# Layer 1's FFN way out by seven block products for eight, in two passes over pairs of F-tiles

## The chip, the cores and the metric

The kernel runs on one core of a Trainium2 chip. The metric is the device time of one execution in microseconds, from the median of three runs. A difference between two kernels is read in per cent of that time.

A core has five engines that work side by side, each with its own queue of instructions, and wait for each other by semaphores: TensorE (PE in the profile, with its weight loads as PEld) multiplies matrices into PSUM, VectorE (DVE), ScalarE (ACT) and GpSimd (POOL) work element by element on SBUF and PSUM, and SyncE (SP) issues the DMA transfers between DRAM and SBUF. PSUM has eight banks of 128 x 512 float32.

## The reference

Two layers of a diffusion backbone over 512 latent tokens and 256 context tokens of width 1024: layer 0 has windowed and dense attention, layer 1 differential attention, and each layer ends with a SwiGLU FFN of hidden width 2816. Only the last step of layer 1 is concerned here, where the context tokens have dropped out:

```python
def _swiglu(h, w_in, w_out):
    gate, up = jnp.split(h @ w_in, 2, axis=-1)
    return (jax.nn.silu(gate) * up) @ w_out
...
        x = x + gx2 * _swiglu(_rms(x, norm_ffn_w[l]) * (1.0 + scx2) + shx2, ffn_w_in[l], ffn_w_out[l])
```

The way out is the product with `w_out`: 512 tokens x 2816 hidden columns by 2816 x 1024, in float32.

## The kernel before

Float32 products run as three products of the matrix engine's fp32r type. Every operand is cut into a high part, which ScalarE casts, and a low part, which VectorE (or GpSimd) makes by subtracting the high part from the operand; then high x high, high x low and low x high are added up in PSUM. `split_into` (L961) makes such a pair: a cast (L963) and a subtraction (L964). `unit` (L360) does the same for a weight that it loads (L364, L369, L370).

The hidden width is cut into NF = 22 F-tiles of 128. In layer 1, `gate_up_blocks` (L818) makes the hidden activations, transposed, F-tile by F-tile. It already multiplies blocks in the Winograd way: seven block products P1 to P7 of 256 tokens by half the model width for eight, whose operands are the blocks B11, B21, B12, B22 of the normed input (in the two `hT` tiles) and the combinations T1 to T4 (T1 in the pool `hop`, T2 and T3 in the former context room, T4 in the place of B12). In each F-tile the order on the matrix engine is P1, P5, P4 of the F-tile before, P6, P2, P7, P3; the last F-tile's P4 ends the stage. Weight tiles `wr`, and the combinations `ws` in PSUM, are cut into `wbh` and `wbl` (L866, L876), nine of each in a ring; of the subtractions, GpSimd makes G2's low part (L876) and S3 (L852), VectorE the rest. The product of gate and up (L929) is written into `hid`, a tile of four F-tiles by 512 tokens; all six such tiles stay in SBUF.

`way_out1` (L1014) then runs over the 22 F-tiles once. For each, `ready_hid` (L1022) loads 128 x 1024 of `ffn_w_out`, cuts it into `wdh` and `wdl` and cuts the hidden F-tile into `hdh` and `hdl`. The first two F-tiles are cut into the places of B11, B21 and T2, which come free while the last F-tile of the gate/up blocks still runs; the others have five buffers. `sums` (L1037) adds up the F-tile's part of all eight output tiles (four token tiles by two halves of the width), each in a PSUM bank of its own: 8 x 3 = 24 matmuls (L1041, L1042, L1043) of 128 x 128 by 512 columns. The last four F-tiles are held back and run bank by bank, so that `residual` (L469: times the gate, L472, plus x, L473) and the store (L1056) of one bank lie beside the products of the next.

The order on the matrix engine is written out by hand (`manual_schedule`); on all other engines a planner with a cost model of its own orders the instructions of the whole program ahead of time, by the order in which the code names them and by when it thinks them ready. `behind(...)` puts an instruction behind a named earlier one in that order. Pools are taken in stack order; a new pool's tiles wait, tile by tile, for those whose memory they take.

Of the kernel before, what the change touches and what calls it, by code (L numbers as in the profile page):

```python
# [18 lines left out]
P = 128  # L19
# [43 lines left out]
def backbone(es: ExitStack, tc: tile.TileContext, x, c, ctx, c_ctx, mod_w, mod_b, norm_mix_w, norm_ffn_w,  # L63
# [25 lines left out]
    def raw_tile(shape, name):  # L89
        return keep.tile(shape, F32, name=name, tag="raw", bufs=2)  # L90
# [24 lines left out]
    def f32(ap):  # L115
        return ap.bitcast(F32)
# [698 lines left out]

        return first_raw

    def gate_up_blocks(l, N, H, order, first_raw, next_raw, ring, ahead, early, tmp, deep, hid, singles, z, after, done=None):  # L818

        raw, sums, ops, psum, tmps = {}, {}, {}, {}, {}  # L820

# [58 lines left out]
        def bank(f, i):  # L880
            if (f, i) not in psum:
                b = i if isinstance(i, int) else i[0]
                psum[f, i] = z("pz") if b == 2 else singles.pool.tile([P, 512], F32, name=f"p{b}", tag=f"p{b}", bufs=2)
            return psum[f, i]

        def product(f, p):
# [21 lines left out]
            def gates():  # L908
                if (f, "cg") not in tmps:
                    tmps[f, "cg"] = tmp.tile([P, 2 * N], F32, name="cg", tag="cg", bufs=deep)  # L910
                return tmps[f, "cg"]

            if p == "P1":
                copied("s1")
            elif p == "P5":
                copied("s5")
            elif p == "P6":
                copied("s2")
            elif p in ("P2", "P3"):
                a, s = (0, "s1") if p == "P2" else (1, "s2")  # L920
                nc.vector.tensor_add(gates()[:, a * N:(a + 1) * N], ps, tmps[f, s])
# [39 lines left out]
    def split_into(to, src):  # L961
        hi, lo = to
        nc.scalar.copy(hi, src)  # L963
        nc.vector.tensor_sub(lo, src, f32(hi))  # L964
# [46 lines left out]
                residual(xs[t], banks[i], g[0 if t < NTX else 1], n)  # L1011
                done(t, n)

    def way_out1(xs, hidr, pool, places_w, places_h):  # L1014

        banks = [p_1.tile([P, 512], F32, name="dps", tag=tag) for tag in ("tr0", "tr1", "acc0", "acc1")]
        banks += [singles.pool.tile([P, 512], F32, name="dps", tag=tag, bufs=2) for tag in ("p0", "p0", "p1", "p1")]
        places = [(t, n) for t in range(NTX) for n in range(2)]
        held = 4
        ready = {}  # L1020

        def ready_hid(f):  # L1022
            def views(raw):
                yield raw, ffn_w_out[1, f * P:(f + 1) * P, :]
            if f < len(places_w):
                raw = raw_tile([P, D], "wdr")
                turn["load"] = nc.sync.dma_start(raw, ffn_w_out[1, f * P:(f + 1) * P, :])
                w, h = places_w[f], places_h[f]
                split_into(w, raw.rearrange("p (k c) -> p k c", k=4))
                split_into(h, hidr[f].rearrange("p (k c) -> p k c", k=2))  # L1030
            else:
                w = [z.rearrange("p (k c) -> p k c", k=4) for z in unit(pool, views, [P, D], 5, "wd")]
                h = [pool.tile([P, 2, SEQ // 2], F32R, name=name, tag=name, bufs=5) for name in ("hdh", "hdl")]
                split_into(h, hidr[f].rearrange("p (k c) -> p k c", k=2))
            ready[f] = h, w

        def sums(f, i):  # L1037
            (t, n), ps = places[i], banks[i]
            hh, hl = (z[:, t // 2, t % 2 * P:(t % 2 + 1) * P] for z in ready[f][0])
            a, b = (z[:, 2 * n:2 * n + 2, :] for z in ready[f][1])  # L1040
            nc.tensor.matmul(ps, hh, a, start=f == 0, stop=False)  # L1041
            nc.tensor.matmul(ps, hh, b, start=False, stop=False)  # L1042
            nc.tensor.matmul(ps, hl, a, start=False, stop=f == NF - 1)  # L1043

        g = gate_row(1, 5, 0, pool)
        for f in range(NF - held):
            ready_hid(f)
            for i in range(len(places)):
                sums(f, i)
        for f in range(NF - held, NF):  # L1050
            ready_hid(f)
        for i, (t, n) in enumerate(places):
            for f in range(NF - held, NF):
                sums(f, i)
            residual(xs[t], banks[i], g, n)
            nc.sync.dma_start(out[0, t * P:(t + 1) * P, n * 512:(n + 1) * 512], xs[t][:, n * 512:(n + 1) * 512])  # L1056

    class Pairs:

# [355 lines left out]
    with tc.manual_schedule(engines={mybir.EngineType.PE}):  # L1415
# [101 lines left out]
        states[0].close()  # L1517
        at.close()
        low = Pool("hid_low")
        hidr = {}  # L1520
# [33 lines left out]
    singles = Pool("singles1", space=PSUM)  # L1554
    high = Pool("hid_high")
    first.append(slot("first1", high, (P, 4, 4, P), F32R))
    ring = Pool("ring1")
    hop = Pool("hop1")
    tmp = Pool("tmp1")
    half = SEQ // 2  # L1560

    def hid_group(f):
        new = slot("hid", high if f in (0, 16, 20) else low)
        hidr.update({f + j: new[:, j] for j in range(4)})

    tc2 = ctx_room([P, KT, TOK - SEQ], F32R, "hTt")
    t1 = [hop.pool.tile([P, 4, half], F32R, name=f"t1{j}") for j in range(2)]
# [31 lines left out]

    with tc.manual_schedule(engines={mybir.EngineType.PE}):  # L1600
        gate_up_blocks(1, half, H, block_order(last_norm, differences, last_difference), first_raw, next_raw, ring.pool, 9, early,
                       tmp.pool, 2, hid_room, singles, acc_tile, "scaled2")
        tmp.close()
        hop.close()
        ring.close()
        g2 = Pool("g2")
        way_out1(xs, hidr, g2.pool, [H["B11"], H["B21"]],
                 [[z[:, 2 * j:2 * j + 2] for z in H["T2"]] for j in range(2)])
    g2.close()
    high.close()  # L1610
    low.close()
# [58 lines left out]
```

## Time and profile before

| | us |
|---|---|
| median of 3 runs | 1728.59 |
| runs | 1728.57 to 1735.44 |
| profiled execution | 1730.63 |
| its span, first to last instruction | 1728.5 |
| granted clock of the matrix engine, mean | 0.989 |
| way out of layer 1, first to last product | 1604.4 to 1724.1 |

In the rows of the profile an instruction stands with its line, its engine and `out<-in` by the names of tiles. Rows of a stretch (A:B, then the length) give the busy time and number of instructions of each engine, in the order of the header row: PE, PEld, DVE, ACT, POOL, then the granted clock of the matrix engine, the mean busy share of the DMA engines and GB/s. Rows of groups give shapes, a count, the busy time, the mean duration in ns, and the idle time before them with what ended it. Rows of a timeline give start and duration in us, and in brackets the idle time before. Rows of one line give count, and shortest, median and longest duration in ns.

### The profile page before, as it was taken

Reading aid. Unit: us, or ns where it says so; the run is one execution under the profiler, and the core shown is the slowest. Engines: PE = TensorE matmul, PEld = TensorE weight load, DVE = VectorE, ACT = ScalarE, POOL = GpSimd, SP = SyncE. Lnnn points to the kernel's source line nnn. Section 1 sums busy time; section 2 is a strip of 40 time slices with the busy share of each in tenths; the row PEclk is TensorE's granted clock in tenths of the full one; section 3 lists DMA queues with packets and bytes.
Section 4 is the critical chain, followed back from the end, with each engine's and each line's share of the span. In section 5 each row is a group of like instructions: output and inputs, shape, how many; then the busy total and the mean of one; then the engine's idle time right before and its main releaser. Section 6 shows DMA issues by size and latency. Waiting matters only on the chain. (4 is left out here: it accounts for less than half of the span.)

```text
span 1728.5 us, 28553 instructions
## 1 busy us (share of the span) xinstructions
PE 1661.1 (96%) x10378; PEld 1478.9 (86%) x10378; DVE 1134.9 (66%) x1993; ACT 936.2 (54%) x2010; POOL 720.8 (42%) x867
## 2 busy tenths in 40 slices
PE   6999999999999999999999899999997999999998
PEld 3887777677999999998777789999986799999887
DVE  3765655534899887757766656666675398887433
ACT  5555655734555665545564456666664465555321
POOL 1774554723345554303413466666653242222000
PEclk8999999999999999999999999999999999999999
DMA  9112322401355555449945212111113143332431
GB/s 319 53 42 62 96 88 82 147 28 51 116 172 174 167 158 158 130 123 345 299 153 172 99 44 75 41 45 46 34 37 98 32 143 102 106 107 57 137 96 67
DMA packets 217964, 194.64 MB, mean 113 GB/s; under 512 B 20000, under 2 KB 202592, under 8 KB 217824
## 3 DMA queue, kind: packets, MB, share of 16 engines
q1 hardware_dynamic: 217472, 192.62, 36.2%
q8 instruction: 81, 1.33, 0.3%
q14 instruction: 59, 0.48, 0.1%
q10 hardware_dynamic: 352, 0.21, 0.0%
HBM read 179.91 MB, written 12.87 MB: 112 GB/s over the span
## 5 line engine op out<-in xcount | busy, mean ns | idle before, releaser
L866 ACT CAST wbh<-wr 128x512 fp32r<-128x512 f32 x170 | 105.1, 621 | 132.9 <-PE p L898 72.1
L898 PE MATMUL p<-hT,wbh 128*128 128x256 f32 (+1 forms) x752 | 156.0, 301 | 0.0
L465 PE MATMUL inps<-wih,hT 128*128 128x384 f32 x384 | 136.1, 354 | 6.5 <-ACT qkv L667 6.0
L876 POOL TENSOR_TENSOR wbl<-wr,wbh 128x512 fp32r<-128x512 f32 x43 | 59.2, 1376 | 174.6 <-ACT wbh L866 170.7
L467 PE MATMUL inps<-wih,hT 128*128 128x384 f32 x384 | 131.3, 342 | 0.0
L466 PE MATMUL inps<-wil,hT 128*128 128x384 f32 x384 | 130.9, 341 | 0.0
L898 PEld LDWEIGHTS p<-hT,wbh 128*128 128x128 f32 x752 | 123.1, 192 | 0.2
L876 DVE TENSOR_TENSOR wbl<-wr,wbh 128x512 fp32r<-128x512 f32 x127 | 106.1, 844 | 20.0 <-ACT wbh L866 16.5
L898 PE MATMUL p<-hT,wbl 128*128 128x256 f32 (+1 forms) x376 | 112.9, 300 | 1.8 <-POOL wbl L876 1.8
L898 PE MATMUL p<-t,wbh 128*128 128x384 f32 (+1 forms) x480 | 111.0, 317 | 0.0
L370 POOL TENSOR_TENSOR wil<-wir,wih 128x768 fp32r<-128x768 f32 x44 | 82.4, 1873 | 51.7 <-ACT wih L369 51.0
L230 POOL TENSOR_TENSOR modp<-modp 128x512 f32<-128x512 f32 x40 | 55.9, 1398 | 115.1 <-ACT modp L229 115.1
L898 PE MATMUL p<-hTt,wbh 128*128 128x256 f32 (+1 forms) x480 | 101.3, 303 | 0.0
L852 POOL TENSOR_TENSOR wr<-wr 128x512 f32<-128x512 f32 x40 | 61.1, 1528 | 92.7 <-DVE ws L857 84.8
L898 PE MATMUL p<-b,wbh 128*128 128x384 f32 x368 | 94.7, 339 | 0.2 <-DVE c L926 0.2
L866 ACT CAST wbh<-ws 128x512 fp32r<-128x512 f32 x120 | 69.6, 581 | 43.2 <-PE p L898 29.2
L595 POOL TENSOR_SCALAR Pt<-Pt,rc 128x256 f32<-128x256 f32 (+3 forms) x96 | 69.3, 734 | 55.8 <-DVE rc L592 48.6
L223 DVE SCALAR_TENSOR_TENSOR ma<-modw,cols,ma 128x256 f32<-128x256 f32 x140 | 89.7, 641 | 2.3
L465 PEld LDWEIGHTS inps<-wih,hT 128*128 128x128 f32 x384 | 72.6, 189 | 12.7 <-ACT qkv L667 8.5
L585 ACT ACTIVATE Pt<-sc,nm 128x256 f32<-128x256 f32 (+3 forms) x96 | 67.8, 711 | 28.7 <-DVE nm L581 14.8
L898 PEld LDWEIGHTS p<-t,wbh 128*128 128x128 f32 x480 | 82.9, 189 | 0.0
L876 DVE TENSOR_TENSOR wbl<-ws,wbh 128x512 fp32r<-128x512 f32 x120 | 81.6, 680 | 1.7 <-ACT wbh L866 1.6
(332 smaller groups left out, 5277.2 us busy)
## 6 DMA issues: line engine op xcount, KB each, us to landing
modw<-in_mod_w_dram SPq DMA_DIRECT2D x96, 512.0 KB, 4.6
wr<-in_ffn_w_in_dram SPq DMA_DIRECT2D x176, 256.0 KB, 3.0
wdr<-in_ffn_w_out_dram SPq DMA_DIRECT2D x66, 512.0 KB, 4.1
wir<-in_od_w_in_dram SPq DMA_DIRECT2D x96, 128.0 KB, 2.3
hidm<-hid SPq DMA_DIRECT2D x44, 192.0 KB, 4.0
hr<-hidm SPq DMA_DIRECT2D x22, 192.0 KB, 4.0
x<-in_x_dram SPq DMA_DIRECT2D x8, 512.0 KB
wir<-in_ev_w_in_dram SPq DMA_DIRECT2D x16, 256.0 KB, 3.3
```

Of the source, the lines that this page charges most:

```text
L223: nc.vector.scalar_tensor_tensor(acc, w[:, k], scale[k], acc, ALU.mult, ALU.add)
L230: nc.gpsimd.tensor_add(pr[:, 0:2], pr[:, 0:2], pr[:, 2:4])
L370: (sub or nc.vector).tensor_sub(lo, raw, f32(hi))
L465: nc.tensor.matmul(ps, hs[0][:, k, :], a, start=k == 0, stop=False)
L466: nc.tensor.matmul(ps, hs[0][:, k, :], b, start=False, stop=False)
L467: nc.tensor.matmul(ps, hs[1][:, k, :], a, start=False, stop=k == KT - 1)
L585: turn["exp"] = nc.scalar.activation(p[:, :n], s, AF.Exp, bias=nm[:, c1], accum_out=sm[:, c1])
L595: nc.gpsimd.tensor_scalar(p[:, :n], p[:, :n], rc[:, hh:hh + 1], 1.0, ALU.mult, ALU.mult)
L852: nc.gpsimd.tensor_sub(w, raw[f, "G1"], w)
L866: nc.scalar.copy(hi, w)
L876: (nc.gpsimd if name == "G2" else nc.vector).tensor_sub(lo, raw[need[n]], f32(hi))
L898: nc.tensor.matmul(ps, w[:, k, :], H[b][h][:, k, :], start=first and k == 0 and q == 0, stop=final and k == 3 and q == 2, skip_group_check ...
```

## The change

`way_out1` is written anew. Each step takes a pair of F-tiles (f and f + 2 within a group of four; 20 and 21 as the last), so there are 11 pairs. A pair is a product of a 2 x 2 block matrix of hidden activations (256 tokens x 128) with a 2 x 2 block matrix of weights (128 x 512), done with seven block products. Each block product is two token tiles by three matmuls of 512 columns.

Eight PSUM banks do not hold seven accumulators of two tiles, so there are two passes over the pairs. The first pass sums P1, P2, P7 and P5 (24 matmuls a step), two banks each. Then P1's banks are copied out and go on as P6's, P7's as P4's, and P5's as P3's, and the second pass adds these three (18 matmuls a step). The last three pairs of the second pass are held back and run bank by bank.

The operands are combinations of blocks. Hidden: `hid_pair` makes two differences per group of four in the `hid` tile itself, on GpSimd, right after every fourth F-tile of the gate/up blocks (`paired`), for the last pair in the way out; `hid_first` makes one more combination on GpSimd and one on VectorE, `hid_second` one on VectorE, each for two pairs at once, and both cut the blocks. Weights: `weights_first` loads both F-tiles of a pair (2 x 512 KB), makes two differences of 512 columns on GpSimd (`d`, which is kept, and one in place), and cuts 4 x 512 columns; `weights_second` loads the second F-tile again (512 KB), makes two differences on GpSimd, and cuts 3 x 512 columns. `cut_into` casts on ScalarE and subtracts on VectorE. There are three places for cut weights (B11 with B21, a new tile pair, B12 with B22) and two for cut hidden blocks (T2 with T3, and a new one); operands are named two steps ahead. `first_parts` finishes, in the second pass at steps 3 and 5, the outputs that need only the first pass, with four GpSimd operations each. The pools `ring` and `hop` change places in the stack.

```diff
                     nc.vector.tensor_mul(hid(f), gates(), bank(f, 0)[:, :2 * N])
+                    if paired and f < NF - 1:
+                        paired(f)
...
+    def hid_pair(f):
+        m = 2 if f % 4 == 3 else int(f == NF - 1)
+        if m:
+            a11, a21, a22 = (groups[f // 4][:, k:k + m, th:th + half] for k, th in ((0, 0), (0, half), (m, half)))
+            nc.gpsimd.tensor_sub(a21, a11, a21)
+            nc.gpsimd.tensor_sub(a21, a22, a21)
...
+        def cut_into(place, k0, src, lo=nc.vector):
+            hi, low = (z[:, k0:k0 + src.shape[1]] for z in place)
+            nc.scalar.copy(hi, src)
+            lo.tensor_sub(low, src, f32(hi))
+
+        def hid_first(q):
+            grp, m = groups[q], min(2, n - 2 * q)
+            a, b = places_h[q % 2]
+            cut_into(a, 0, grp[:, 0:2 * m, 0:half])
+            s = sums_tile(q)
+            nc.gpsimd.tensor_add(s[:, 0:m], grp[:, 0:m, half:], grp[:, 0:m, 0:half])
+            nc.vector.tensor_sub(s[:, m:2 * m], grp[:, m:2 * m, half:], grp[:, 0:m, half:])
+            cut_into(b, 0, s[:, 0:2 * m])
...
+        def hid_second(q):
...
+            cut_into(a, 0, grp[:, 0:2 * m, half:])
+            s = sums_tile(q, True)
+            nc.vector.tensor_sub(s[:, 0:m], grp[:, m:2 * m, 0:half], grp[:, 0:m, half:])
+            cut_into(b, 0, s[:, 0:m])
...
+        def weights_first(i):
+            f, f2 = pairs[i]
+            place = places_w[i % 3]
+            own = i in (0, 3, 6)
+            if own:
+                up, down = (raw_tile([P, 2, 512], "wdr") for _ in range(2))
             else:
...
+                raw = raws[i % 3 - 1 if i < 7 else (i + 1) % 2]
+                up, down = raw[:, 0:2], raw[:, 2:4]
+            with behind(*(("load",) if i else ())):
+                load(up.rearrange("p a c -> p (a c)"), f)
+            load(down.rearrange("p a c -> p (a c)"), f2)
+            d = diff_tile(i)
+            diffs.append(d)
+            if own:
+                cut_into(place, 0, flat(up[:, 0:1]))
+                cut_into(place, 4, flat(down[:, 0:1]))
+            nc.gpsimd.tensor_sub(d, up[:, 1:2], up[:, 0:1])
+            turn["diff"] = nc.gpsimd.tensor_sub(up[:, 1:2], down[:, 1:2], up[:, 1:2])
+            if own:
+                cut_into(place, 2, flat(up[:, 1:2]))
+            else:
+                cut_into(place, 0, flat(raw[:, 0:3]))
+            cut_into(place, 6, flat(d))
...
+        def weights_second(i):
+            place = places_w[(n + i) % 3]
+            raw = raws[i % 2][:, i // 2 % 2 * 2:i // 2 % 2 * 2 + 2]
+            load(raw[:, 0:2].rearrange("p a c -> p (a c)"), pairs[i][1])
+            d = diffs[i]
+            nc.gpsimd.tensor_sub(d, raw[:, 1:2], d)
+            nc.gpsimd.tensor_sub(raw[:, 0:1], raw[:, 0:1], d)
+            cut_into(place, 4, flat(d))
+            cut_into(place, 0, flat(raw[:, 0:2]))
...
+            elif p == "P6":
+                s1, s7 = late["s1"][:, t], late["s7"][:, t]
+                nc.scalar.copy(s1, ps)
+                nc.vector.tensor_mul(s7, s1, gs[1])
+                nc.vector.tensor_mul(s1, s1, gs[0])
+                nc.gpsimd.tensor_add(cols_of(t, 1), cols_of(t, 1), s7)
+                nc.vector.tensor_add(cols_of(t + 2, 0), cols_of(t + 2, 0), s1)
+                nc.gpsimd.tensor_add(cols_of(t + 2, 1), cols_of(t + 2, 1), s7)
+                store(t + 2, 1)
...
+        def first_parts(t):
+            s1, s7 = late["s1"][:, t], late["s7"][:, t]
+            nc.vector.tensor_add(s1, banks["P2"][t], s1)
+            for a, b, tt in ((s1, 0, t), (s7, 1, t + 2)):
+                nc.gpsimd.tensor_mul(a, a, gs[b])
+                nc.gpsimd.tensor_add(cols_of(tt, b), cols_of(tt, b), a)
+            store(t, 0)
...
+        for k in range(2 * n):
+            prepare(k + ahead)
+            second, i = divmod(k, n)
+            order = ("P6", "P4", "P3") if second else ("P1", "P2", "P7", "P5")
+            if second and i >= n - held:
+                continue
+            if second and i in (3, 5):
+                first_parts(i // 4)
+            for p in order:
+                for t in range(2):
+                    product(p, i, t)
...
+    ring = Pool("ring1")
     hop = Pool("hop1")
-    ring = Pool("ring1")
```

More of the change, by code (lines that the diff above doesn't have):

```diff
@@ L816, in raw_quarters, with gate_up_blocks @@
         return first_raw
-    def gate_up_blocks(l, N, H, order, first_raw, next_raw, ring, ahead, early, tmp, deep, hid, singles, z, after, done=None):
+    def gate_up_blocks(l, N, H, order, first_raw, next_raw, ring, ahead, early, tmp, deep, hid, singles, z, after, done=None, paired=None):
         raw, sums, ops, psum, tmps = {}, {}, {}, {}, {}
@@ L1012, in way_out0 @@
                 done(t, n)
[L1014 to L1030, printed above, removed]
-            else:
[L1032 to L1043, printed above, removed]
-        g = gate_row(1, 5, 0, pool)
[L1046 to L1056, printed above, removed]
@@ L1519, in backbone @@
         low = Pool("hid_low")
-        hidr = {}
+        hidr, groups = {}, []
         def slot(name, pool, shape=(P, 4, SEQ), dtype=F32):
@@ L1556, in backbone @@
     first.append(slot("first1", high, (P, 4, 4, P), F32R))
+    hop = Pool("hop1")
     ring = Pool("ring1")
-    hop = Pool("hop1")
     tmp = Pool("tmp1")
@@ L1564, in hid_group @@
         hidr.update({f + j: new[:, j] for j in range(4)})
+        groups.append(new)
     tc2 = ctx_room([P, KT, TOK - SEQ], F32R, "hTt")
```

101 lines of the change are left out of this document (97 added, 4 removed).

## The prediction

> **What bounds the kernel now.** I read the page's busy shares first, then busy time by stretch of the span, then the groups of instructions of the last stretch with shapes kept apart, then the chain in order of time, and last the timelines of VectorE and GpSimd in layer 1's gate/up blocks, where both work at once.
>
> ```profile
> span 1728.5 us, 28553 instructions
> PE 1661.1 (96%) x10378; PEld 1478.9 (86%) x10378; DVE 1134.9 (66%) x1993; ACT 936.2 (54%) x2010; POOL 720.8 (42%) x867
> ```
> ```profile
> core 0: us, PE busy (x) PEld busy (x) DVE busy (x) ACT busy (x) POOL busy (x), PEclk, DMA share, GB/s
> 1604.40:1724.10 119.70, 119.68 (x528) 98.73 (x527) 48.23 (x55) 30.93 (x40) 0.00 (x0) 1.00 0.30 101
> 1440.00:1600.00 160.00, 160.00 (x1335) 160.00 (x1334) 134.06 (x202) 89.19 (x174) 37.62 (x29) 1.00 0.32 93
> ```
> ```profile
> 1599.92 4.45 PE p L898 x36
> 1604.37 0.23 PE dps L1041
> ...
> 1723.85 0.24 PE dps L1043
> 1724.11 0.71 DVE dps L472
> 1724.85 0.69 DVE x L473
> ```
>
> The page says that the matrix engine (PE) is busy 96% of the span. The first row by stretch is the way out: 528 products in 119.7 us without a hole, 0.2267 us each, clock 1.00, VectorE (DVE) busy 40% and GpSimd (POOL) never. The chain says the same: PE from 1604.37 to 1724.09, then 1.4 us of VectorE and a store. So in this stage PE is the bound, and fewer products are worth 0.2267 us each as long as their operands come in time. What making operands costs today:
>
> ```profile
> L370 DVE TENSOR_TENSOR wdl<-wdr,wdh 128x1024 fp32r<-128x1024 f32 x20 | 24.5, 1226 | 8.1 <-ACT wdh L369 8.1
> L369 ACT CAST wdh<-wdr 128x1024 fp32r<-128x1024 f32 x20 | 20.9, 1047 | 5.5 <-DMA wdr<-in_ffn_w_out_dram 5.5
> L963 ACT CAST hdh<-hid 128x512 fp32r<-128x512 f32 x20 | 12.2, 622 | 57.5 <-PE dps L1042 57.5
> ```
> ```profile
> 1605.08 1.22 DVE L370 TENSOR_TENSOR wdl<-wdr,wdh 128x1024 fp32r<-128x1024 f32 x1
> 1606.22 0.69 DVE L964 TENSOR_TENSOR hdl<-hid,hdh 128x512 fp32r<-128x512 f32 x1
> ```
>
> Successive VectorE subtractions start 1.14 us apart at 1024 columns (1605.08 to 1606.22), less than the 1.22 us one lasts.
>
> **GpSimd and VectorE take turns.** The change puts GpSimd to work throughout this stage, so what matters is what both cost together. The way out shows nothing of it; the gate/up blocks do. `wr`, `wbh`, `hid` and `cg` lie in SBUF, `ws`, `pz` and `p` in PSUM.
>
> ```profile
> 488.05 0.69 DVE L857 TENSOR_TENSOR ws<-wr 128x512 f32<-128x512 f32 x1
> 488.65 2.39 DVE L876 TENSOR_TENSOR wbl<-wr,wbh 128x512 fp32r<-128x512 f32 x2
> ```
> ```profile
> 488.87 1.62 POOL L852 TENSOR_TENSOR wr<-wr 128x512 f32<-128x512 f32 x1 [5.62 <-DVE ws L857]
> ```
> ```profile
> 1446.50 1.30 POOL L876 TENSOR_TENSOR wbl<-wr,wbh 128x512 fp32r<-128x512 f32 x1 [6.80 <-ACT wbh L866]
> 1448.49 1.30 POOL L852 TENSOR_TENSOR wr<-wr 128x512 f32<-128x512 f32 x1 [0.69 <-DVE ws L857]
> ```
> ```profile
> 1446.74 1.61 DVE L857 TENSOR_TENSOR ws<-wr 128x512 f32<-128x512 f32 x1
> 1448.27 0.68 DVE L876 TENSOR_TENSOR wbl<-ws,wbh 128x512 fp32r<-128x512 f32 x1
> 1448.87 0.41 DVE L921 TENSOR_TENSOR cg<-pz,s 128x256 f32<-128x256 f32 x1
> 1449.37 0.96 DVE L876 TENSOR_TENSOR wbl<-wr,wbh 128x512 fp32r<-128x512 f32 x1
> ```
>
> A GpSimd operation runs from 1446.50 to 1447.80. VectorE's `ws<-wr`, two inputs in SBUF, starts at 1446.74 and ends at 1448.35: 0.55 us after GpSimd is done, although the same form takes 0.69 us undisturbed (488.05). The next GpSimd operation lasts until 1449.79; `wbl<-wr,wbh` ends at 1450.33, again 0.54 us behind it, while `wbl<-ws,wbh` and `cg<-pz,s`, with one input in PSUM, pass untouched. At 488 it is the other way round: a VectorE subtraction started at 488.65 and by its 0.69 us ends at 489.34; GpSimd, issued at 488.87, ends at 490.49, 1.15 us later, and VectorE's second one at 491.04, 0.55 us after that. So two-input SBUF work of the two engines excludes each other for the whole instruction. Prices per 512 columns when both queues are full: GpSimd 1.15 us, VectorE 0.55 us behind a GpSimd turn and 0.60 us behind its own (488.05 to 488.65).
>
> **The change, part by part.**
>
> *Products.* 7 of 8 block products: 462 instead of 528, 66 × 0.2267 = 15.0 us less. A step of the first pass (4 products × 2 tiles × 3 = 24) takes PE 5.44 us, one of the second (18) 4.08 us.
>
> *First pass, two steps* (two pairs, one hidden group). GpSimd: `d` and `up` for each step and one sum of hidden halves, 5 × 512 columns = 5 × 1.15 = 5.75 us. VectorE, all with both inputs in SBUF: per step the low parts of 1536 and of 512 columns (1.14 + 0.54 = 1.68, and 0.60), and for the group 1024, 512 and 1024 (1.14, 0.60, 1.14): 2 × 2.28 + 2.88 = 7.44, less 0.05 for each of 5 that follow a GpSimd turn, 7.19. Together 12.94 us, where PE wants 10.88. Either engine alone would fit; taking turns they don't. Times 5.5 (eleven steps): 71.2 us.
>
> *The last pair's two hidden differences* between the passes, 256 columns each on GpSimd: half a unit each, 1.2 us.
>
> *Second pass, two steps.* GpSimd 4 × 1.15 = 4.60. VectorE 2 × (0.60 + 1.14) + 1.14 + 0.60 + 0.60 − 4 × 0.05 = 5.62. Together 10.22 us against PE's 8.16. Times 5.5: 56.2 us.
>
> *`first_parts`*: 8 GpSimd operations of 512 columns, put in steps 3 and 5 of the second pass, ahead of the last weights: 8 × 1.15 = 9.2 us.
>
> The two engines so owe 137.8 us of turns before step 10 of the second pass has its operands.
>
> *Ahead of the handover.* Step 0's raw weights go to tiles that are free early, T2 is free after P6 and T3 after P7 of the last F-tile. Step 1's raw tile lies where T1 was, free after P5. These rows show how soon such places were filled before:
>
> ```profile
> 1597.80 0.62 ACT L963 CAST hTt<-hid 128x512 fp32r<-128x512 f32 x1 [1.79 <-PE p L898]
> ```
> ```profile
> wdr<-in_ffn_w_out_dram SPq DMA_DIRECT2D x20, 512.0 KB, 3.5
> ```
>
> The cast into T2 began 6.6 us before the handover at 1604.4. I take step 0 as made by then (3 × 1.15 on GpSimd, 0.60 + 2 × 1.14 + 4 × 0.60 = 5.3 on VectorE) and step 1's two GpSimd subtractions (2.3): 11.0 us done ahead. If VectorE is kept busy by the last F-tile and only GpSimd works ahead, 5.
>
> *The end.* The last three steps are held and run bank by bank, so P6 can do two of its three (6 products) before it needs step 10; 48 × 0.2267 = 10.9 us come after it. Of the 137.8 some 0.6 us (P3's hidden part) are wanted only later. PE so ends 137.8 − 11.0 − 0.6 + 10.9 = 137.1 us after the handover, for 119.7 before: **+17.4 us**.
>
> *Casts without cover.* Where no other step has turns to take, a cast stands bare: 1.6 us at step 1's first cut (1.05 + 0.52) and 1.1 us within step 10's two. **+2.7 us.**
>
> *Costed at nothing.* (1) The ten GpSimd subtractions of `paired` in the gate/up blocks. The 29 GpSimd operations of 1440 to 1600 are 37.6 us of 160 and VectorE is 84% busy, so 40 us have 6.5 us spare for 2.3 us of turns more; GpSimd waits there for VectorE's `hid` with the next `wbl` of G2 behind it, and the weight ring is nine deep. Without that cover up to 10 × 1.15 = 11.5 us. (2) ScalarE: per two first steps 2 × (1.57 + 0.62) + 2 × 1.05 = 6.5 us of 13. (3) The loads: 33 of 512 KB for 22, 1 MB per 6.5 us, 161 GB/s; 512 KB landed in 3.5 us. From step 7 on, two raw tiles serve the first pass: landing of both halves (at most 7.0), two GpSimd turns with a cut between (4.0), cast 1.6, cut 1.7 make 14.3 us per two steps against 12.9, so 2.7 us over steps 7 to 10 at worst. SP's queue holds each load until its tile is free, and only later loads and stores stand behind it. (4) P1's and P7's copies and P5's adds read PSUM and have other products beside them; the swapped order of the pools moves no instruction. (5) The tail: the same 1.4 us of VectorE and one 256 KB store; P6's follow-up (2 × (0.62 + two products, three adds)) has P4's and P3's 8.2 us beside it.
>
> **Sum.** −15.0 us of products, and in their place a wait for operands of 35.1: +20.1 us. The profiled execution took 1730.63 us (span 1728.5), so it would take 1751; the median of the runs shown, 1728.59, is 2.0 us below it and the change starts from that: 1749.
>
> A figure against this. The Trainium skill (SBUF — State Buffer, "SBUF: two separate sides") gives GpSimd's port 614 GB/s; by it a two-input operation of 512 columns (2 × 262 KB) would take an estimated 0.85 us, the 58.5 GpSimd units (27.5 + 1 + 22 + 8) 18 us less, and the sum +2 us. The rows have 1.15 us in a turn and 1.30 us alone, so I use theirs.
>
> **Rivals.**
>
> *PE stays the bound (faster).* If what VectorE and GpSimd read at the same time cost no turns, a step has VectorE 3.7 and GpSimd 3.2 us beside PE's 5.44, and all is hidden: 1728.6 − 15.0 + up to 3 us at the handover = 1714 to 1717. It decides from where the two engines together fall below 10.88 us for two steps, 16% under my 12.99. Against it: every two-SBUF row above that meets GpSimd.
>
> One GpSimd line, with its shortest, median and longest duration in ns:
>
> ```profile
> L852 POOL TENSOR_TENSOR wr<-wr x40: 1289/1612/2732, 447.8 to 1579.5; 128x512 f32<-128x512 f32 x40
> ```
>
> *GpSimd's turn is shorter.* At 1.15 − 20.1 / 58.5 = 0.81 us per 512 columns the change is even; 1728 to 1734. For it only that page's port figure above; against it, the forty subtractions of that row, the shortest 1.29.
>
> *The steps don't overlap.* If each engine's queue is so ordered that a step's chain (two subtractions 2.3, cast 1.6, cut 1.7, small cut 0.6, half a group: 1.44 + 0.58 of turns and 1.05 of casts) runs without another step's turns in its holes, a first step takes 9.3 us for 6.5, 11 × 2.8 = +31 us on the first pass alone: 1780. For it: queues in order, two raw tiles; against it: loads and places reach two steps ahead.
>
> **How the numbers follow.** One more stretch, with the columns of the first such rows, shows what a pause does to PE's clock:
>
> ```profile
> 984.00:990.00 6.00, 4.71 (x18) 4.71 (x19) 3.79 (x8) 2.04 (x5) 3.12 (x6) 0.72 0.47 131
> ```
>
> Turns bind: 0.80, 1749 us, itself 1735 to 1770. Low end: `first_parts` slips behind the last weights (−9.2), every cut follows a turn (−1.4), and the bare casts are covered (−2.7): +6.8, 1735. High end: GpSimd at the 1.30 us it takes alone (+8.8), VectorE never 0.05 less (+2.5), 5 us ahead for 11 (+6.0), the raw tiles (+2.7) and a slow clock behind the last pause (+1.7): +41.8, 1770. The last comes from that row, where PE pauses for 1.3 us in 6 and has 0.72 of its clock, 1.7 us lost; at earlier pauses PE waits anyway. The chances of the others: no overlap 0.08, PE bound 0.07, short GpSimd turn 0.05. Within 0.5% (8.6 us), about what a measurement can tell from no change: the short turn and the lowest edge of the likeliest, 0.07. Faster by more: 0.07. Slower by more: 0.86. The range leaves out the first and third rival and reaches from 1735 to 1770.
>
> **What would show it.** Right: in the way out GpSimd busy over half, VectorE's two-input cuts of 1024 columns longer than 1.22 us by up to 1.2, GpSimd's 512 columns longer than 1.30; PE idle some 2 us per two steps, before an even step most, released by VectorE's cuts; 462 products over about 140 us; first pass longer than 60 us by about 10. Wrong: VectorE's cuts at 1.14 us beside a busy GpSimd; PE waiting for DMA; PE's holes only at the handover; holes in the gate/up blocks, where the rows above have none.

## The result and the profile after

The changed kernel took 1759.21 us (median, 1754.95 to 1760.63) where the kernel before took 1728.58 beside it: ratio 1.0164, 95% interval 1.0133 to 1.0195. The ratio is that of the means of four runs each (1758.5 and 1730.1), so it is slower by 28 us. A second measurement, on another chip, gave 1.0150 (1.0124 to 1.0177), 26 us. The profiled execution took 1758.79 us.

First the page of the changed kernel: its span and each engine's busy time.

```profile
span 1757.0 us, 28664 instructions
PE 1656.2 (94%) x10312; PEld 1469.5 (84%) x10312; DVE 1225.4 (70%) x2037; ACT 963.1 (55%) x2046; POOL 858.5 (49%) x941
```

Then busy time by stretch (PE, PEld, DVE, ACT, POOL, clock, DMA share, GB/s): from where the way out began in the kernel before to where it begins now, its first and second pass, the whole way out, and the gate/up stretch of the prediction.

```profile
1604.37:1611.79 7.42, 4.80 (x31) 4.59 (x29) 6.09 (x6) 2.48 (x4) 3.74 (x2) 0.79 0.22 71
1611.79:1679.00 67.21, 62.30 (x264) 50.30 (x264) 65.39 (x42) 31.10 (x37) 50.93 (x28) 0.97 0.49 172
1679.00:1750.37 71.37, 53.66 (x201) 40.85 (x199) 70.36 (x54) 26.45 (x37) 54.03 (x31) 0.88 0.22 68
1611.79:1750.37 138.58, 115.96 (x463) 91.16 (x462) 135.75 (x95) 57.54 (x74) 104.96 (x58) 0.92 0.35 118
1440.00:1600.00 160.00, 160.00 (x1336) 160.00 (x1335) 137.53 (x206) 89.16 (x174) 55.86 (x39) 1.00 0.32 94
```

The way out has 462 products for 528 and takes 138.6 us, from the start of its first to the end of its last; by the same measure the kernel before took 119.9 (1604.21 to 1724.08). TensorE was idle for 22.6 of them, and its products, 104.7 us at the 0.2267 us of before, took 116.0 at a mean clock of 0.92. VectorE now shows 136 of 139 us busy and GpSimd 105, waits for a turn included. The gate/up stretch is as full as before, 160.00 of 160.00, although GpSimd shows 18 us more in it, waits for a turn included.

The groups of the way out, shapes apart (busy us, mean ns), show what makes VectorE so busy.

```profile
L1060 DVE TENSOR_TENSOR hT<-wt,hT 128x512 fp32r<-128x512 f32 x12 | 16.9, 1410 | 0.0
L1060 DVE TENSOR_TENSOR hT<-wdr,hT 128x1024 fp32r<-128x1024 f32 x8 | 15.1, 1892 | 0.5 <-ACT hT L1059 0.5
...
L1060 DVE TENSOR_TENSOR wdl<-wdr,wdh 128x1536 fp32r<-128x1536 f32 x4 | 8.8, 2208 | 1.4 <-ACT wdh L1059 1.4
...
L1101 POOL TENSOR_TENSOR wdr<-wdr 128x512 f32<-128x512 f32 x10 | 20.3, 2030 | 1.6 <-DMA wdr<-in_ffn_w_out_dram 1.0
...
L1115 POOL TENSOR_TENSOR wdr<-wdr,wt 128x512 f32<-128x512 f32 x9 | 15.4, 1713 | 0.5
```

A 1024-column cut takes 1.89 us for 1.23, a 512-column one 1.41 for 0.69, and GpSimd's subtraction 1.7 to 2.0 for 1.30. The timelines of VectorE and of GpSimd at one place show why.

```profile
1676.22 1.78 DVE L1078 TENSOR_TENSOR hs<-hid 128x512 f32<-128x512 f32 x1
1677.93 1.77 DVE L1060 TENSOR_TENSOR hT<-u,hT 128x512 fp32r<-128x512 f32 x1
1679.62 2.28 DVE L1060 TENSOR_TENSOR hT<-wdr,hT 128x1024 fp32r<-128x1024 f32 x1
```
```profile
1675.71 1.75 POOL L1114 TENSOR_TENSOR wt<-wdr,wt 128x512 f32<-128x512 f32 x1
1677.54 1.62 POOL L1115 TENSOR_TENSOR wdr<-wdr,wt 128x512 f32<-128x512 f32 x1
1679.11 1.71 POOL L1114 TENSOR_TENSOR u<-wdr,u 128x512 f32<-128x512 f32 x1
```

The ends are what to read. GpSimd ends at 1677.46, VectorE at 1678.00 (0.54 us later), GpSimd at 1679.16 (1.16), VectorE at 1679.70 (0.54), GpSimd at 1680.82 (1.12). Each runs alone in its turn, at the prices that the prediction read from the gate/up blocks. (The opening section names PSUM for all three elementwise engines together; in the traces of this case no GpSimd instruction has an operand in PSUM, and these turns concern operands in SBUF only.)

TensorE's waits from the last gate/up products to the end (us in total, times, longest):

```profile
PE dps L1126 <- DVE hT L1060: 7.5, 5, 2.5
PE dps L1125 <- DVE s L1146: 6.1, 1, 6.1
PE dps L1125 <- ACT u L1142: 5.7, 1, 5.7
PE p L898 <- DVE p L926: 2.6, 1, 2.6
PE dps L1126 <- DVE wdl L1060: 1.9, 2, 1.5
PE dps L1125 <- ACT hT L1059: 1.0, 1, 1.0
PE dps L1127 <- DVE hd L1060: 0.5, 1, 0.5
```

No wait is for a DMA. Two, 11.8 us together, are for P1's copy (L1142) and P5's add (L1146) at the change of passes. The fourth lies ahead of the handover; VectorE's timeline has its cause.

```profile
1603.94 1.35 DVE L1060 TENSOR_TENSOR hTt<-hid,hTt 128x1024 fp32r<-128x1024 f32 x1
1605.22 1.78 DVE L1060 TENSOR_TENSOR hT<-wdr,hT 128x512 fp32r<-128x512 f32 x1
1606.92 1.74 DVE L1060 TENSOR_TENSOR hT<-u,hT 128x512 fp32r<-128x512 f32 x1
1608.59 0.42 DVE L926 TENSOR_TENSOR p<-p,s 128x256 f32<-128x256 f32 x1
```

P7's add of the last F-tile (L926), for which P4 waits, stands behind three cuts of the new step 0, two of them stretched by GpSimd's turns. What GpSimd makes there is for later steps, as its timeline shows: step 0's two weight differences were made 170 us earlier, inside the gate/up blocks, and those of step 1 come here.

```profile
1435.01 1.74 POOL L1100 TENSOR_TENSOR u<-wdr 128x512 f32<-128x512 f32 x1
1436.83 1.61 POOL L1101 TENSOR_TENSOR wdr<-wdr 128x512 f32<-128x512 f32 x1
```
```profile
1602.91 1.30 POOL L1100 TENSOR_TENSOR u<-wdr 128x512 f32<-128x512 f32 x1 [9.10 <-DMA wdr<-in_ffn_w_out_dram]
1604.29 2.16 POOL L1101 TENSOR_TENSOR wdr<-wdr 128x512 f32<-128x512 f32 x1
```

The same timeline at the end of the way out, two instructions of P6's follow-up, which take 0.69 us by themselves:

```profile
1742.27 1.68 DVE L1153 TENSOR_TENSOR x<-x,u 128x512 f32<-128x512 f32 x1
1743.87 1.77 DVE L1150 TENSOR_TENSOR s<-u,g 128x512 f32<-128x512 f32 x1
```

From the two traces the 28.5 us by which the span grew come to this: +1.0 up to the last gate/up product of layer 1 ahead of `npt`, the transposes of the last normed token tile (1380.77 to 1381.77; the kernel before differs there by 2.4 between two profiles of its own); +1.9 from there to the 58th product behind it, with `npt` in between (10.2 to 12.1); +4.7 from that 58th product to the handover (213.2 to 217.9); +18.7 in the way out; +2.2 behind the last product (4.45 to 6.64).

### The profile page after: what moved, and what is told of

Its sections match the earlier page's. It is cut to its first block, busy times and chain, and to the rows that moved or that the text cites. A ratio compares the mean times of both kernels' runs of the same rounds, so it can differ in the third digit from the quotient of the medians.

```text
span 1757.0 us, 28664 instructions
## 1 busy us (share of the span) xinstructions
PE 1656.2 (94%) x10312; PEld 1469.5 (84%) x10312; DVE 1225.4 (70%) x2037; ACT 963.1 (55%) x2046; POOL 858.5 (49%) x941
## 5 line engine op out<-in xcount | busy, mean ns | idle before, releaser
L465 PEld LDWEIGHTS inps<-wih,hT 128*128 128x128 f32 x384 | 72.0, 188 | 12.7 <-ACT qkv L667 8.4
```

The costliest lines, as they stand in the source:

```text
L465: nc.tensor.matmul(ps, hs[0][:, k, :], a, start=k == 0, stop=False)
```

## The experiments

All are told as ratios to the kernel before on the same chip, with 95% intervals. Their theory T is the prediction's: turns of GpSimd and VectorE set the end of the way out. Q is its rival: the order of the queues and single waits set it, and GpSimd's work costs VectorE nothing.

### All of the way out's GpSimd work on VectorE (e1_vector)

```diff
-            nc.gpsimd.tensor_sub(d, up[:, 1:2], up[:, 0:1])
+            nc.vector.tensor_sub(d, up[:, 1:2], up[:, 0:1])
...
-                nc.gpsimd.tensor_mul(a, a, gs[b])
+                nc.vector.tensor_mul(a, a, gs[b])
```

This was done for all GpSimd lines of `hid_first`, `weights_first`, `weights_second`, `after` and `first_parts`, nine in all.

> All nine GpSimd lines of the way out go to VectorE; nothing else is edited. Theory T (turns: VectorE's and GpSimd's operations with two inputs in SBUF exclude each other, and the sum of their turns sets when operands are ready): VectorE owes 5.5 x (7.44 + 5 x 0.60) + 1.2 + 5.5 x (5.82 + 4 x 0.60) + 8 x 0.60 = 109 us of work for 138 us of turns, 29 us less, so about 1730 us (1724 to 1738) for the changed kernel's 1759; 512-column cuts 0.69 us, 1024-column cuts 1.22 us. Theory Q (queues in order: the copies of P1 and the adds of P5 stand behind other work at the pass change, and GpSimd's work costs VectorE nothing): VectorE gets 30 us of work more and its queue runs later, 1759 to 1785 us.

Measured: 1733.44 us, ratio 0.9997 (0.9986 to 1.0009). The stretch of its way out, and two of its groups:

```profile
1608.15:1727.48 119.33, 111.06 (x464) 89.67 (x462) 114.32 (x155) 60.26 (x75) 1.06 (x1) 0.96 0.41 139
```
```profile
L1060 DVE TENSOR_TENSOR hT<-wdr,hT 128x1024 fp32r<-128x1024 f32 x8 | 9.8, 1228 | 0.6 <-ACT hT L1059 0.6
L1060 DVE TENSOR_TENSOR hT<-wt,hT 128x512 fp32r<-128x512 f32 x12 | 8.3, 692 | 0.0
L1060 DVE TENSOR_TENSOR wdl<-wdr,wdh 128x1536 fp32r<-128x1536 f32 x4 | 7.0, 1754 | 0.2 <-ACT wdh L1059 0.2
```

With the same arithmetic, handing an engine's whole work in the way out to an engine that was already the busier one takes 26 to 29 us away (by ratio, from 1.0150 or 1.0164). Between the first profile of the changed kernel and this one, 19.3 of 24.9 us lie in the way out itself. The cuts are back at 1.23 and 0.69 us, GpSimd has one operation left there, and VectorE is busy for 114.3 of 119.3 us. That VectorE is the bound now, and the 66 products less win nothing for that reason, is read from this share; no run takes work off VectorE alone.

### Half of it on VectorE (e8_half), beside the changed kernel again (after_again)

```diff
-            turn["diff"] = nc.gpsimd.tensor_sub(up[:, 1:2], down[:, 1:2], up[:, 1:2])
+            turn["diff"] = nc.vector.tensor_sub(up[:, 1:2], down[:, 1:2], up[:, 1:2])
...
-            nc.gpsimd.tensor_sub(raw[:, 0:1], raw[:, 0:1], d)
+            nc.vector.tensor_sub(raw[:, 0:1], raw[:, 0:1], d)
```

> The changed kernel unedited, on the same chip as the next three, to compare them with. Both theories: 1.3% to 1.9% slower than the kernel before.

> One of the two weight differences of each step goes to VectorE, 22 operations in all; the other stays on GpSimd. Theory T: each saves 1.15 - 0.60 = 0.55 us of turns, 12 us less than the changed kernel (9 to 14). Theory Q: VectorE gets 13 us of work more: 0 to 13 us more.

Measured: the changed kernel 1.0150 (1.0124 to 1.0177); with half of the subtractions moved 1.0095 (1.0074 to 1.0115), 10 us less. By the prices in a turn, 22 operations at 1.15 − 0.60 make 12.1 us. The gain fits T's 9 to 14 us and not Q's loss. Its place fits less well: between the two profiles taken together (9.3 us apart) only 4.3 us lie in the way out (139.4 to 135.0), 2.3 between the 58th product named above and the handover, and 2.0 behind the last product. So the run speaks for turns, but not for the price of each.

### GpSimd kept at work, without reading (e7_memset)

The four subtractions of weights on GpSimd are replaced by two fills each with a constant, so these differences are left out of the computation.

```diff
-            nc.gpsimd.tensor_sub(d, up[:, 1:2], up[:, 0:1])
+            nc.gpsimd.memset(d, 0.5)
+            nc.gpsimd.memset(d, 0.5)
```

> Each of the four GpSimd weight differences is replaced by two fills of the same tile with a constant: GpSimd is still busy in every step, writes the same tiles at the same place of the order, but reads nothing. The differences are left out, so the output is not the reference's. Theory T (only reads exclude): VectorE's cuts of 512 and 1024 columns at 0.69 and 1.22 us beside a filling GpSimd; left are 14.5 GpSimd turns, and the way out falls from 138.6 to between 110 and 120 us: 20 to 28 us less than the changed kernel. Rival Q (it is GpSimd's place in the chain of a step, or the queues' order, that makes PE wait): cuts as short, but PE waits as before, less than 8 us gained. Rival W (any GpSimd instruction takes the port): cuts still 1.7 us.

Measured: 1729.32 us, ratio 0.9981 (0.9966 to 0.9997), 29 us below the changed kernel. Its way out by stretch, then two groups:

```profile
1611.15:1724.91 113.76, 108.27 (x464) 88.40 (x462) 93.37 (x95) 60.41 (x75) 69.70 (x98) 0.97 0.43 144
```
```profile
L1060 DVE TENSOR_TENSOR wdl<-wdr,wdh 128x1536 fp32r<-128x1536 f32 x4 | 7.0, 1758 | 6.5 <-ACT wdh L1059 6.5
...
L1118 POOL MEMSET wdr<- 128x512 f32 x11 | 5.8, 527 | 14.6 <-DMA wdr<-in_ffn_w_out_dram 14.4
```

GpSimd is still busy for 70 us, and VectorE's 1536-column cut takes 1.76 us where it took 2.21 in the changed kernel: what stretches the cuts is that GpSimd reads, not that it works. For the whole 29 us the run is less clean, because two fills are done sooner than a subtraction and read nothing: ScalarE's casts wait for GpSimd for 4.9 us in this way out, for 37.6 in the changed kernel's. In e1_vector, where the differences are still made and waited for, 26 to 29 us went too. With VectorE busy for 93 of 114 us neither engine sets the end any more, and the way out is still 9 us above the 104.7 of its products.

### One GpSimd subtraction twice (e3_double)

```diff
             nc.gpsimd.tensor_sub(d, up[:, 1:2], up[:, 0:1])
+            nc.gpsimd.tensor_sub(d, up[:, 1:2], up[:, 0:1])
```

> The first weight difference of each first-pass step is made twice on GpSimd: 11 operations of 512 columns more, same result. Theory T: 11 turns of 1.15 us, +12.7 us, about 1772 us (1768 to 1775). Theory Q: GpSimd has idle time in every step and VectorE's work is not touched: +0 to +3 us, 1759 to 1762 us.

Measured: 1768.59 us, ratio 1.0201 (1.0184 to 1.0218), where the changed kernel had 1.0164 and 1.0150 in its two measurements: 6 to 9 us more, for the 12.7 that T had. Two of the eleven second subtractions ran ahead of the handover, where they cost nothing that shows. The other nine made the way out 148.3 us long, for 138.6 and 139.4 in the two profiles of the changed kernel: 1.0 to 1.1 us each, close to T's 1.15. A way out bound by single waits would have shown nothing or up to 3 us.

### Copies ahead of the next operands (e2_copies, e5_vector_copies)

By Q the waits at the change of passes come from the order of the queues and are worth their length. The second pass's first operands are put behind P7's copies and P5's adds.

```diff
-                nc.scalar.copy(late["s7"][:, t], ps)
+                turn["p7"] = nc.scalar.copy(late["s7"][:, t], ps)
...
-            prepare(k + ahead)
+            if k == n - 1:
+                hid_second(0)
+            else:
+                with behind("p5", "p7"):
+                    prepare(k + ahead)
```

> Only the order of the queues changes: the operands of the second pass from its step 1 on stand behind P7's copies on ScalarE and P5's adds on VectorE, so that the two waits of PE at the pass change (5.9 and 6.5 us) should go. Theory T: operands are made at the same rate, 96% of the stretch is turns already, so the time is given back at the held steps: 1755 to 1761 us. Theory Q: 12 us less, about 1747 us.

Measured: 1758.52 us, ratio 1.0147 (1.0132 to 1.0162): nothing gained. TensorE's largest waits, of e2_copies:

```profile
PE dps L1126 <- DVE hT L1060: 9.2, 5, 2.5
PE dps L1127 <- DVE hTt L1060: 5.0, 3, 3.9
PE dps L1126 <- DVE wdl L1060: 3.2, 2, 1.6
PE dps L1127 <- DVE hd L1060: 2.9, 2, 2.5
```

The 11.8 us for the copy and the add are gone, and 20.3 us of waits for low parts stand in the trace where 9.9 (7.5, 1.9 and 0.5) stood; the way out took 141.3 us. The waits named where TensorE happened to stand; the turns set when it could end.

The same order was then put on e1_vector.

> e1_vector and e2_copies together. Theory T: 29 us less as in e1_vector, and now the bank waits are no longer hidden behind turns, so their removal counts on top of it: 1714 to 1728 us, possibly below the kernel before. Theory Q: the gain of e2_copies against the loss of e1_vector: 1747 to 1775 us.

Measured: 1740.92 us, ratio 1.0046 (1.0031 to 1.0060). A miss on both sides: it is some 8 us slower than e1_vector. One of VectorE's own waits in e5_vector_copies, and one of TensorE's:

```profile
DVE s L1146 <- PE dps L1127: 3.7, 1, 3.7
```
```profile
PE dps L1126 <- DVE hT L1060: 12.2, 3, 4.9
```

VectorE, the bound, now stands still for 3.7 us until TensorE has P5, with the cuts of the next step behind it in its queue, and TensorE then waits for those cuts. The same order that changed nothing while turns set the end costs some 8 us here, more than the 3.7 us for which VectorE stands still at that place. That the wait is what costs is argued from this row; nothing but the order differs between the two kernels.

### What a later handover costs (e6_handover), and starving at single steps (e9_split, e9b_split_only)

On top of e1_vector, four of step 0's six cuts were put behind P7's add of the last F-tile (the diff shows the first).

```diff
-                nc.vector.tensor_add(tmps[f, "c2"], ps, tmps[f, "s5"])
+                turn["c2"] = nc.vector.tensor_add(tmps[f, "c2"], ps, tmps[f, "s5"])
...
-            cut_into(a, 0, grp[:, 0:2 * m, 0:half])
+            with behind(*(("c2",) if q == 0 else ())):
+                cut_into(a, 0, grp[:, 0:2 * m, 0:half])
```

> e1_vector (all nine GpSimd lines on VectorE) with the cuts of step 0 put behind the last F-tile's P7 addition (L926) in VectorE's queue. In e1_vector the last product of the gate/up blocks waited for that addition behind three cuts, and the way out began 3.9 us later than in the kernel before. Theory T: with the turns gone the handover counts: 2 to 4 us less than e1_vector, ratio to the kernel before 0.997 to 0.999. If the cuts themselves were what the products wait for, no difference: 1.000.

Then, on top of that, steps 1 and 2 were cut in pieces, and in e9_split the second pass's hidden operands were also made earlier.

```diff
-            if own:
+            if own or i in (1, 2):
...
-                if k < n and i % 2 == 0:
+                if k != n and i % 2 == 0:
...
-            if n < k <= len(stages):
-                _, hid, i = stages[k - 1]
-                if i % 2 == 0:
-                    hid(i // 2)
+            if k == n + 1:
+                hid_second(0)
```

> As the run before, but with the second pass's hidden operands where they were: only the cuts of steps 1 and 2 in 512-column pieces. If starvation at the start counts, 3 to 5 us go against the kernel with everything on VectorE (ratio 0.997 to 0.999); if VectorE's total sets the end, the waits come back later and the ratio is 1.000.

> All of the way out's GpSimd work is on VectorE, step 0's cuts stand behind P7's add of the last F-tile, the first operands of steps 1 and 2 are cut in 512-column pieces so that P1 can begin after the first, and from the second group on the second pass's hidden operands are made ahead of the next weights. If what remains after the turns are gone is starvation at single places (PE waited 1.8 and 2.3 us at steps 1 and 2 and 3.1 us at step 4 of the second pass with all work on VectorE), 5 to 10 us go: ratio 0.994 to 0.998 to the kernel before, way out 110 to 114 us. If VectorE's total of some 109 us of cuts sets the end wherever its waits stand, nothing goes: ratio 1.000, way out 118 us.

Measured: e6_handover 1.0007 (0.9992 to 1.0022), e9b_split_only 1.0005 (0.9995 to 1.0016), e9_split 1.0021 (1.0009 to 1.0033). Three edits meant to take waits of 2 to 3 us away, and none gained time; e9_split is even a little slower than the kernel before. TensorE's named waits from 1595 us on came to 8.6 us in e1_vector and to 9.2, 10.8 and 9.9 in these: they moved and did not shrink. One stretch row each, of e6_handover, e9b_split_only and e9_split:

```profile
1606.76:1725.20 118.44, 109.26 (x464) 88.04 (x462) 115.63 (x158) 59.70 (x75) 1.06 (x1) 0.97 0.40 141
```
```profile
1609.17:1729.27 120.10, 109.28 (x464) 87.71 (x462) 115.93 (x161) 60.22 (x79) 1.06 (x1) 0.97 0.41 139
```
```profile
1610.62:1730.40 119.78, 109.83 (x464) 88.31 (x462) 116.48 (x162) 60.15 (x79) 1.06 (x1) 0.97 0.41 139
```

VectorE is busy for 115.6 to 116.5 us in each, some 97% of the stretch, whatever the waits of TensorE are. This came out as the other case of each expectation, and it fits a bound by VectorE's sum of work once GpSimd is out of the scheme.

### The order of the pools (before_again, e10_pools)

The kernel before, profiled on another chip, was to tell whether the later gate/up products belong to the chip.

> The kernel before, unedited, for a profile on this chip: ratio 1.000, way out 119.7 us without a hole. It says how much of the 3 to 6 us by which the experiments reach the gate/up blocks of layer 1 later than the first profile is the chip's and not the change's: if the change's, the first gate/up product of layer 1 starts where the first profile has it; if the chip's, as late as in the experiments.

Measured: ratio 0.9989 (0.9978 to 0.9999), way out 119.87 us. Its 58th product behind the last one ahead of `npt` comes 2.0 us later than in the first profile, but the stretch between these two is not longer: 9.8 us, 10.2 in the first profile. In each of the eleven profiles of kernels with the two pools swapped it was 12.0 to 12.8. ScalarE's timeline of the changed kernel has the place:

```profile
1381.32 0.62 ACT L866 CAST wbh<-wr 128x512 fp32r<-128x512 f32 x1 [0.33 <-DMA wr<-in_ffn_w_in_dram]
1382.15 0.62 ACT L866 CAST wbh<-wr 128x512 fp32r<-128x512 f32 x1 [0.22 <-DMA wr<-in_ffn_w_in_dram]
1383.84 0.62 ACT L866 CAST wbh<-wr 128x512 fp32r<-128x512 f32 x1 [1.07 <-DMA wr<-in_ffn_w_in_dram]
1384.36 1.14 ACT L337 ACTIVATE nroom<-x,rs_n 128x1024 f32<-128x1024 f32 x1
```

`nroom`, for which TensorE's `npt` waits, stands behind three casts where it stood behind two, and the third waits 1.07 us for its load. In SP's queue a load of 512 KB for the way out (L1034) stands ahead of two loads of `wr` that it stood behind before; it is not what the cast waits for, since it was issued at 1384.02, when that cast's own load (issued at 1379.35) had landed. So the swap was undone.

```diff
+    ring = Pool("ring1")
     hop = Pool("hop1")
-    ring = Pool("ring1")
...
+        hop.close()
         ring.close()
-        hop.close()
```

> The kernel with all of the way out's GpSimd work on VectorE (ratio 0.9997), with the two pools ring1 and hop1 opened and closed in the order of the kernel before. In every changed kernel one load of 512 KB (wdr, L1034) stands two places earlier in SP's queue at 1384 us and one more cast of wbh ahead of nroom (L337) in ScalarE's; the changed kernel's nroom starts 1.07 us later behind a late wr, TensorE's npt waits 3.5 us for it where it waited 2.6, and the half-clock stretch behind it is longer. If the swapped pools are what moved these queues, the wait is 2.6 to 2.7 us again, the first products of layer 1's gate/up start 2 to 3 us earlier against the products ahead of them, and the way out stays at 118 to 121 us: ratio 0.9980 to 0.9990. If the order has another origin or the delay is given back later: 0.9995 to 1.0005.

Unlike its expectation says, this kernel moved only the five GpSimd lines that make operands to VectorE and kept the twelve operations of `first_parts` and of P6's follow-up on GpSimd. So it differs from e1_vector in two things. Measured: 1732.70 us, ratio 1.0008 (0.9997 to 1.0019). ScalarE's timeline and TensorE's wait, of e10_pools:

```profile
1378.74 0.62 ACT L866 CAST wbh<-wr 128x512 fp32r<-128x512 f32 x1 [1.18 <-DMA wr<-in_ffn_w_in_dram]
1379.51 0.62 ACT L866 CAST wbh<-wr 128x512 fp32r<-128x512 f32 x1 [0.15 <-DMA wr<-in_ffn_w_in_dram]
1380.04 1.15 ACT L337 ACTIVATE nroom<-x,rs_n 128x1024 f32<-128x1024 f32 x1
```
```profile
PE npt L342 <- ACT nroom L337: 2.6, 1, 2.6
```

Two casts again, 2.6 us as in the kernel before (3.5 in the changed one), and the stretch takes 10.0 us. The third cast is there in the changed kernel and in e1_vector alike, with GpSimd's work and without, and gone in e10_pools; so the swap of the pools moved the queues, and it costs 2.0 to 2.8 us at that place. What this is worth in the whole is not: the way out of e10_pools took 121.5 us and the time behind it 5.7, for 119.3 and 4.7 of e1_vector. The twelve GpSimd operations that were left could account for that (12 × 0.55 = 6.6 us of turns, by the prices above), but no run with the pools alone put back shows it.

No version with the whole computation was measurably faster than the kernel before.

## Why the prediction was right, and where it was short

**The bound changes from TensorE to turns of two engines: right.** From the handover to the product that waits for the last step's low part (1611.8 to 1739.4), either engine has an instruction with two inputs in SBUF for 125.1 of 127.6 us. e1_vector, e8_half and e7_memset each take away a part of what GpSimd reads, and the time falls; a second subtraction in e3_double adds to it. The prices, 1.15 us for GpSimd and 0.55 for VectorE behind it, are in the timeline to 0.03 us.

**The sum of turns: right, to about 1%.** The forecast had 11.0 us done ahead of the handover: step 0, and step 1's two GpSimd subtractions. The trace has just that (GpSimd at 1433 to 1438 and at 1602.9 and 1604.3, VectorE's six cuts and one difference of step 0), and one GpSimd sum more, at 1606.4: 12.2 us by the same prices. Of the 137.8 us the last cut of 1024 columns (1.1 us) turned out to be wanted only later, as it starts at 1739.3, beside the product, while P3's hidden part was made before it. So 137.8 − 12.2 − 1.1 = 124.5 us of turns were left by the forecast's prices, and 125.1 were measured. The bare casts were forecast at 2.7 us at steps 1 and 10; all holes in the turns together are 2.5, of which VectorE's waits for casts are 1.9, at 1653, 1671 and 1737. That size is near, but the places are others; so much of the hit is luck. In all, 126.2 + 2.7 = 128.9 us were forecast from the handover to that product, and it came after 127.6. Behind that product, 10.9 us of products were forecast and 11.0 came.

**The way out, +17.4 and +2.7 for bare casts: +18.7 measured.** Of this, products are −15.0, TensorE idle +22.6, and its slower clock +11.3 (116.0 − 104.7). For the first pass "longer than 60 us by about 10" came 67.2, with a wait of 5.7 behind it. Of TensorE idle "some 2 us per two steps" less came in the first pass: three waits, 4.9 us together. Half of all idle time lies at the change of passes.

**P1's copies and P5's adds "have other products beside them": wrong as a step, without effect on the sum.** They stood in the queues behind operands of the second pass, and TensorE waited 11.8 us. e2_copies shows that the time comes back in other waits while turns set the end.

**What was missing from the sum is ahead of and behind the way out: 8.8 of the 28.5 us.** Three places:
- The handover. The prediction took the work done ahead as free. It isn't: step 0's cuts lie in VectorE's queue ahead of P7's add, and GpSimd's turns for later steps stretch them to 1.78 us. TensorE waits there for 2.6 us, and its products behind that wait come 0.21 us apart for 0.12. From the 58th product named above to the handover the changed kernel took 216.8 to 217.9 us in its two profiles, 213.2 before and 213.2 to 213.9 in the five kernels in which all GpSimd lines of the way out are on VectorE. So the turns cost 3 to 4 us here too, before the first product that they feed.
- "The swapped order of the pools moves no instruction": wrong. It moved a load and a cast; the cast costs 2 us at a place 220 us ahead of the change.
- The tail, "the same 1.4 us of VectorE": 6.6 us for 4.45. VectorE's last adds queue behind P6's follow-up, which GpSimd's turns stretch, so the last store is issued 2.5 us behind the last product, for 1.5 before. That is 1.0 of the 2.2 us; the other 1.2 lie behind the issue of that store, and their cause is open. In e2_copies and e8_half, with the same GpSimd adds, the tail was 4.6, so the moment matters as much.

**`paired` at nothing: right for all but one place.** The gate/up stretch shows TensorE busy for 160.00 of 160.00 us. Ahead of it, at 1437.7, TensorE waits 0.6 us for VectorE; there a `paired` subtraction and GpSimd's three operations for step 0 stand one behind the other. **The loads at nothing: right.** TensorE waits for no DMA in the way out. GpSimd does, for 19 us, but the turns have only 2.5 us of holes, so VectorE had work of its own meanwhile.

**The rivals.** "PE stays the bound" (whose 12.99 us per two steps is the 12.94 of the sum) would have needed GpSimd and VectorE to read at the same time; with most of the reads taken out, e7_memset came to 1729, so 1714 to 1717 was too low for it: single waits and the slow clock remained. "GpSimd's turn is shorter" falls by the 1.12 to 1.16 us of the timeline. "The steps don't overlap" would have shown a first pass of 102 us (11 steps of 9.3); it took 67. The port figure of the Trainium skill (SBUF — State Buffer, "SBUF: two separate sides"), by which 0.85 us was estimated for a GpSimd turn, doesn't fit the timeline's 1.12 to 1.16; that the two engines exclude each other is what the timelines and e7_memset's cuts show.

Still open: what the 2 us of the pools are worth in the whole, and why the stretch around 1304 to 1317, where the attention ends, varied by 3 to 4 us among profiles of the changed kernel and its variants.

## What to carry to other kernels

Add up what VectorE and GpSimd read from SBUF with two inputs as if one engine did it, before work is handed to the idle one of them: here GpSimd's 512 columns cost 1.15 us of VectorE's time, and on VectorE itself they would have cost 0.60. A wait in a trace says where an engine stood, not what it would gain without it: as long as an engine's sum is the bound, a wait that is removed comes back elsewhere (e2_copies), and an order that makes that engine itself wait loses time (e5_vector_copies, some 8 us). An edit of memory places alone can reorder queues far ahead of it, so compare the order of every queue, not only that of the code that was edited.

## What the runs showed of the hardware beside this

Fills do not take turns: with GpSimd fills of 0.53 us beside each of the four for 0.6 to 1.6 us, VectorE's 1536-column cut kept the 1.75 us that it takes alone (1.758 in e7_memset, 1.754 in e1_vector). The Trainium skill (SBUF — State Buffer, "SBUF: two separate sides") names only a GpSimd operation that reads SBUF as one that blocks VectorE's work with two SBUF inputs; the run agrees.

TensorE's waits came with a slower clock, worth half as much again or more: in the way out 22.6 us of idle time, in pieces of 0.4 to 6.1 us, came with 11.3 us of slower products at a mean clock of 0.92; in e1_vector 8.3 us idle came with 6.4 us at 0.96. No run varies the waits alone.
